# Modulations of the first layer summed on VectorE, and output weights split among the first projections: a two-layer hybrid attention and state-space block on one core

## The chip, the cores and the metric

The kernel runs on one core of a Trainium2 chip. The core has TensorE (matmuls into eight PSUM banks), VectorE, ScalarE and GpSimd, and queues on which transfers are issued. The metric is the device time of one execution in microseconds (us). TensorE's clock has two levels, 1.2 and 2.4 GHz; the profile gives the granted share of the higher one.

## The reference

A trunk of two layers works on 512 latent tokens (stream 0) and 256 context tokens (stream 1) of width 1024, side by side as 768 columns. Cut to what matters here:

```python
for l in range(DEPTH):                        # 2 layers
    m  = split(silu(c)     @ w_mod[l] + b_mod[l], 6)   # six modulations of 1024 for the latent tokens
    mc = split(silu(c_ctx) @ w_mod[l] + b_mod[l], 6)   # and six for the context tokens
    p  = modulate(rmsnorm(h,  g_norm1[l]), m[0],  m[1])  @ w_in[l]
    pc = modulate(rmsnorm(hc, g_norm1[l]), mc[0], mc[1]) @ w_in[l]
    oa, ob, om, od = neighbourhood(p, pc), sliding_window(p, pc), latent_attention(p, pc), state_space(p, pc)
    h  = h + m[2] * (concat(oa, ob, om, od) @ w_out[l])
    h  = h + m[5] * (square(relu(modulate(rmsnorm(h, g_norm2[l]), m[3], m[4]) @ w_mlp1[l])) @ w_mlp2[l])
    # the context stream hc goes the same way with mc, but not in the last layer
```

The weights `w_mod[l]` are 1024 x 6144 and `w_out[l]` is 1024 x 1024. So the modulations are two vectors (latent and context) times a large matrix, done once a layer. The first layer's m[0] and m[1] are needed before its first projection; m[2] is needed at the output projection, m[3] to m[5] in the MLP.

## The kernel before

**Matmuls in three products.** Every large fp32 matmul is done with split operands: a weight tile of 128 x 1024 (`wr`) is copied to a rounded high part by ScalarE (`wh`, L238) and the rest is subtracted by VectorE (`wl`, L239). `dense` (L250) then runs high x high, high x low and low x high on TensorE (L258). The pool of weights has three buffers each of `wr`, `wh` and `wl`; a load on SyncE's queue (SP) starts when its buffer is free.

**Stages of a layer.** After the first norm come the first projections (`ckv`, `cq` 0 and 1, `sq` 0), the latent queries and keys, and then three merges of generators, in which heads and projections take turns by numbers: latent heads with six more projections; sliding-window heads with the convolutions; the state-space scan with the neighbourhood heads and the first half of the output projection. Then comes the second half of the output projection, the second norm, and the MLP in four quarters of eight up blocks and eight down blocks. In the first layer the first projections run from 58.5 to 145.4 us, the latent heads to 212, the sliding-window heads to 350, scan and neighbourhood heads to about 470, and the MLP from some 500 to 1000 us. The order on each engine is set by a scheduler from the order of the program.

**Modulations.** Those of the first layer that its first norm needs, columns 0 to 2047, are made at the start by `first_mod`, which the change doesn't touch. The others of the first layer (columns 2048 to 6143) are `mod_steps(0)`: two groups of 2048 columns, eight steps each. A step loads two tiles of 128 x 1024 into the weight pool (L169, tag `wr`, shared with the projections) and multiplies them with the activated conditions on TensorE, into one bank that a group holds over its eight steps (L172). At the eighth step the bank is copied by ScalarE, transposed by TensorE and added to the bias. Steps stand in a list, `todo`; `more()` does the next of them: after each projection (`in_proj`, L705), while over `KEEP[0]` = 2 are left, and the last two in the merge with the scan. The second layer's modulations are made in the first layer's MLP by `mod_sums(1)` in another way: a chunk of 768 columns at a time, VectorE multiplies a weight tile with the condition of each of the two streams and adds it to one of two sums, over eight tiles (L206 for the first, L208 for the rest), and TensorE closes the chunk by multiplying the sums with ones (L212), a copy by ScalarE (L215) and three transposes (L221).

**Output weights ahead.** `split_ahead(l)` loads the eight blocks of `w_out[l]` (`wr`), splits them, and writes both parts by GpSimd's queue to a scratch in DRAM, `oscr` (L505). `wh` and `wl` are free when the writes have landed. In the first layer these eight are a third generator in the sliding-window merge; for the second layer they stand at the end of `todo`, behind all sums of modulations, in the first layer's MLP.

## Time and profile before

| | |
|---|---|
| median of 3 runs | 1813.32 us (1809.08 to 1813.66) |
| the profiled execution, its own time | 1818.32 us |
| its span | 1816.5 us |
| TensorE busy (share of the span) | 1756.8 us (97%) |
| VectorE busy | 1110.4 us (61%) |
| ScalarE busy | 737.2 us (41%) |
| GpSimd busy | 237.9 us (13%) |
| moved by DMA | 238.94 MB, mean 132 GB/s |

Busy time is the sum over an engine's instructions of one profiled execution. In the rows below PE is TensorE, PEld its weight loads, DVE VectorE, ACT ScalarE, POOL GpSimd and SP SyncE; a q behind a name is the queue of its instructions. "x8" counts instructions that the view has put together, and a bracket at the end of a row tells the idle time before it and what ended that. A name like `wl<-wr,wh` is the tile written and the tiles read. Times of rows are us from the start of the span.

### The profile page before, as it was taken

How to read it: one execution, taken by the hardware profiler on the slowest of the kernel's cores; microseconds unless marked ns; L12 is line 12 of the kernel's file. 1: busy time of each engine (PE TensorE's matmuls, PEld its weight loads, DVE VectorE, ACT ScalarE, POOL GpSimd, SP SyncE). 2: the span in 40 equal slices, each digit the busy share in tenths (PEclk: the TensorE clock that was granted, in tenths of full speed). 3: DMA queues.
4: the chain of work that ended last, by engine and by line, in shares of the span. 5: the costliest groups of instructions: out<-in, count | busy, mean ns of one | idle time of the engine just before them, and what ended most of it. 6: DMA issues, size and time to landing. Idle time of an engine off the chain costs nothing.

```text
span 1816.5 us, 28898 instructions
## 1 busy us (share of the span) xinstructions
PE 1756.8 (97%) x11170; PEld 1498.3 (82%) x11170; DVE 1110.4 (61%) x2372; ACT 737.2 (41%) x1497; POOL 237.9 (13%) x367
## 2 busy tenths in 40 slices
PE   8999999999989999999999999999989999999998
PEld 7877867777878888888887998688867898888888
DVE  5448448688677566557554675657778663434345
ACT  4347546655344123123114543555544451323244
POOL 0102012134320000000001331100024300000002
PEclk8999999999989999999999999999999999999999
DMA  9440267632634444434348643111233543332333
GB/s 334 137 151 18 65 209 238 211 123 83 209 111 137 141 129 131 119 106 140 109 124 298 191 128 125 47 36 36 91 122 116 200 139 94 102 94 93 103 101 121
DMA packets 86249, 238.94 MB, mean 132 GB/s; under 512 B 9200, under 2 KB 17392, under 8 KB 86112
## 3 DMA queue, kind: packets, MB, share of 16 engines
q1 hardware_dynamic: 74976, 208.57, 36.6%
q0 software_dynamic: 7104, 24.33, 3.7%
q10 hardware_dynamic: 4032, 4.20, 0.7%
q8 instruction: 88, 1.44, 0.3%
q14 instruction: 49, 0.40, 0.1%
HBM read 214.52 MB, written 22.54 MB: 131 GB/s over the span
## 4 chain that ended last, share of the span: by engine, by line
PE 62%; issue 26%; DVE 5%; DMA 3%; ACT 2%; POOL 1%; SPq 0%; DVEq 0%; ACTq 0%; POOLq 0%
PE pt L258 42%; PE pt L476 4%; PE pt L470 3%; PE pS L663 2%; PE pS L428 2%; PE pS L415 2%; PE pt L172 1%; PE pt L663 1%; PE pt L293 1%; PE pt L930 1%; PE pS L1028 1%; DMA wr<-in_w_mlp_dram 1%; PE pt L861 1%; DVE wl L239 1%; ACT wh L238 0%
## 5 line engine op out<-in xcount | busy, mean ns | idle before, releaser
L238 ACT CAST wh<-wr 128x1024 fp32r<-128x1024 f32 x206 | 215.8, 1048 | 424.4 <-PE pt L258 302.6
L239 DVE TENSOR_TENSOR wl<-wr,wh 128x1024 fp32r<-128x1024 f32 x206 | 254.1, 1234 | 116.6 <-ACT wh L238 101.0
L258 PE MATMUL pt<-ah,wh 128*128 128x512 f32 (+1 forms) x1304 | 276.4, 354 | 5.8 <-ACT ah L343 2.8
L258 PE MATMUL pt<-ah,wl 128*128 128x512 f32 (+1 forms) x1304 | 269.0, 348 | 2.3 <-DVE wl L239 2.3
L258 PE MATMUL pt<-al,wh 128*128 128x512 f32 (+1 forms) x1304 | 269.2, 347 | 0.0
L258 PEld LDWEIGHTS pt<-ah,wh 128*128 128x128 f32 x1304 | 214.1, 191 | 45.3 <-ACT ah L343 4.0
L258 PEld LDWEIGHTS pt<-ah,wl 128*128 128x128 f32 x1304 | 215.1, 191 | 34.1 <-DVE wl L239 2.7
L258 PEld LDWEIGHTS pt<-al,wh 128*128 128x128 f32 x1304 | 213.4, 191 | 31.0 <-issue 1.9
L258 PE MATMUL pt<-hh,wh 128*128 128x256 f32 (+1 forms) x896 | 168.8, 330 | 0.0
L258 PE MATMUL pt<-hl,wh 128*128 128x256 f32 (+1 forms) x896 | 167.0, 329 | 0.0
L258 PE MATMUL pt<-hh,wl 128*128 128x256 f32 (+1 forms) x896 | 166.9, 329 | 0.0
L1281 DVE SCALAR_TENSOR_TENSOR h<-pt,mod,h 128x512 f32<-128x512 f32 (+1 forms) x112 | 66.4, 597 | 153.8 <-PE pt L258 153.6
L258 PEld LDWEIGHTS pt<-hh,wh 128*128 128x128 f32 x896 | 137.7, 189 | 18.5 <-issue 1.9
L258 PEld LDWEIGHTS pt<-hh,wl 128*128 128x128 f32 x896 | 138.1, 190 | 15.4
L258 PEld LDWEIGHTS pt<-hl,wh 128*128 128x128 f32 x896 | 138.1, 190 | 15.0
L208 DVE SCALAR_TENSOR_TENSOR ma<-wm,cact,ma 128x768 f32<-128x768 f32 x112 | 110.5, 1015 | 61.9 <-DMA wm<-in_w_mod_dram 61.8
L1271 ACT ACTIVATE r<-pt 128x512 f32<-128x512 f32 (+1 forms) x101 | 51.3, 508 | 222.0 <-PE pt L258 220.4
L1273 DVE TENSOR_TENSOR r<-r 128x512 f32<-128x512 f32 (+1 forms) x101 | 58.2, 578 | 123.1 <-ACT r L1271 123.0
L319 POOL TENSOR_TENSOR sq<-sq,sq 128x256 f32<-128x256 f32 x66 | 65.0, 985 | 431.7 <-ACT sq L315 431.1
L452 ACT ACTIVATE pr<-pr,m 128x512 f32<-128x512 f32 (+2 forms) x96 | 77.8, 811 | 45.9 <-DVE m L438 45.2
L258 PE MATMUL pt<-oh,wo 128*128 128x256 f32 (+1 forms) x576 | 95.9, 311 | 0.0
L258 PEld LDWEIGHTS pt<-oh,wo 128*128 128x128 f32 x576 | 81.1, 199 | 5.6 <-issue 1.9
(295 smaller groups left out, 2472.3 us busy)
## 6 DMA issues: line engine op xcount, KB each, us to landing
wr<-in_w_mlp_dram SPq DMA_DIRECT2D x154, 512.0 KB, 3.5
wo<-oscr SPq DMA_DIRECT2D x66, 512.0 KB, 4.6
wm<-in_w_mod_dram SPq DMA_DIRECT2D x80, 384.0 KB, 3.6
wr<-in_w_a_dram SPq DMA_DIRECT2D x36, 512.0 KB, 4.2
wm<-in_w_mod_dram SPq DMA_DIRECT2D x32, 512.0 KB, 4.2
wr<-in_w_out_dram SPq DMA_DIRECT2D x16, 512.0 KB, 4.2
oscr<-wh POOLq DMA_DIRECT2D x16, 512.0 KB, 4.6
oscr<-wl POOLq DMA_DIRECT2D x16, 512.0 KB, 6.0
```

The costliest lines, as they stand in the source:

```text
L208: V.scalar_tensor_tensor(a[:, :T], w, cact[:, k, i:i + 1], a[:, :T], ALU.mult, ALU.add)
L238: A.copy(wh, raw)
L239: low.tensor_tensor(wl, raw, wh.bitcast(F32), ALU.subtract)
L258: PE.matmul(ps[:, :n], w[:, k - k0, :], acts[k][a][:, c0:c0 + n], start=i == 0, stop=i == len(mm) - 1)
L319: G.tensor_tensor(sq[0][:, :n], sq[0][:, :n], q[:, :n], ALU.add)
L452: A.activation(pr[:, :off], src, AF.Exp, scale=-1.0 if tabs else sgn, bias=mcol, accum_out=s2[:, a:a + 1])
L470: PE.transpose(pt[:, i * P:(i + 1) * P], probs[a][:, (g0 + i) * P:(g0 + i + 1) * P], ident)
L476: last_mm = PE.matmul(pv[64 * a:64 * a + 64, :P], vt(a, t), pts[a][:, t * P:(t + 1) * P], start=t == 0, stop=t == nkt - 1)
L663: PE.matmul(acc[t], acts[k][a][:, t * P:(t + 1) * P], slabs[pc][w][:, kk, :], start=k == 0 and x == 0, stop=k == KD - 1 and x == 2)
L1271: A.activation(r[:, :n], ps, AF.Relu)
L1273: V.tensor_tensor(r2[:, :n], r[:, :n], r[:, :n], ALU.mult)
L1281: V.scalar_tensor_tensor(h[d][:, c0:c0 + n], ps, mod[:, 40 + d, s:s + 1], h[d][:, c0:c0 + n], ALU.mult, ALU.add)
```

## The change

**Sums instead of matmuls.** The first layer's other modulations (columns 2048 to 6143) are no longer steps of matmuls. `mod_steps` is gone, and `mod_sums` takes a first block: `mod_sums(0, 16)` has five chunks of 768 columns and a last one of 256, each of eight steps of sums on VectorE and the transposes as a ninth. In the first layer its weight tiles and sums are in the large pool `u` (40 buffers, shared with activations), in the second layer as before. After every projection `more(MPROJ)` does three entries of the list instead of one; what is left of it is done ahead of the neighbourhood tables, and no longer in the merge with the scan.

**Output weights.** The first layer's eight splits leave the sliding-window merge. Two each stand behind the projections `ckv`, `cq` 0, `cq` 1 and `sq` 0. The second layer's splits no longer stand behind all its sums: one follows every chunk.

```diff
-    def mod_steps(l):
...
-                        w = wp.tile([P, 1024], F32, tag="wr", name=nm("wm"))
-                        nc.sync.dma_start(w, D["w_mod"][l, k * P:(k + 1) * P, c0:c0 + 1024])
...
-                        PE.matmul(box["ps"][32 * g:32 * g + 32, :], cact[:, k, :],
-                                  ws[g // 2][:, (g % 2) * 512:(g % 2) * 512 + 512],
-                                  start=k == 0, stop=k == KD - 1)
...
+    def mod_sums(l, b0=0):
+        for at in range(b0, 48, 6):
+            nb = min(6, 48 - at)
...
+                    w = (wp.tile([P, T], F32, tag="wr", name=nm("wm")) if l else unit("u", nm("wm")))[:, :W]
+                    nc.sync.dma_start(w, D["w_mod"][l, k * P:(k + 1) * P, at * P:at * P + W])
                     if k == 0:
+                        box.extend(unit("pT" if l else "u", nm("ma"))[:, :W] for _ in range(2))
                     for i, a in enumerate(box):
                         if k == 0:
+                            V.tensor_scalar(a, w, cact[:, k, i:i + 1], None, ALU.mult)
                         else:
+                            V.scalar_tensor_tensor(a, w, cact[:, k, i:i + 1], a, ALU.mult, ALU.add)
...
-    todo = mod_steps(0)
+    todo = mod_sums(0, 16)
...
         def in_proj(g, i, sg, fn):
             dense(D["w_a"][l, BLK[g, i]], acts, sg, fn)
-            if len(todo) > KEEP[l]:
-                more()
+            more(MPROJ)
...
+        ahead = split_ahead(0) if l == 0 else []
+
+        def some():
+            for _ in range(2):
+                if ahead:
+                    ahead.pop(0)()
         proj("ckv", 0)
+        some()
         proj("cq", 0)
+        some()
         next(latent)
         proj("cq", 1)
+        some()
...
         proj("sq", 0)
+        some()
...
-              (calls(*[lambda i=i: conv(i) for i in range(6)], lambda: gate_z(0), lambda: gate_z(1)), CONVN[l]),
-              (calls(*(split_ahead(0) if l == 0 else [])), 11))
-        more(len(todo) - KEEP[l])
+              (calls(*[lambda i=i: conv(i) for i in range(6)], lambda: gate_z(0), lambda: gate_z(1)), CONVN[l]))
+        more(len(todo))
...
-        merge((ssd(), SSDN[l] + na_), (na(), na_), (calls(*outa), OUTN[l]), (calls(*[more] * len(todo)), MODN[l]))
+        merge((ssd(), SSDN[l] + na_), (na(), na_), (calls(*outa), OUTN[l]))
...
-            todo.extend(mod_sums(l + 1))
-            todo.extend(split_ahead(l + 1))
+            sums, ahead = mod_sums(l + 1), split_ahead(l + 1)
+            for i in range(0, len(sums), 9):
+                todo.extend(sums[i:i + 9])
+                todo.append(ahead.pop(0))
```

**VectorE, first projections of the first layer.** Before, from the split of the second query projection (`wl_883`, the weights of `cq` 1) to that of the next projection (`wl_1021`, those of `sq` 0). Between them are an eviction of the first query projection (`cq`) and the small steps of an inverse root (`ss`, `rs`, `rsv`, `rsq`):

```order
L239 TENSOR_TENSOR wl_883<-wr_880,wh_882 128x1024
L373 COPY cq_783<-pt_816 128x256
L296 TENSOR_SCALAR ss_867<-pt_860 128x6
L279 TENSOR_SCALAR rs_869<-ss_867 128x6
L280 SCALAR_TENSOR_TENSOR rsv_870<-rs_869 128x6
L281 TENSOR_TENSOR rsv_870<-rsv_870,ss_867 128x6
L282 SCALAR_TENSOR_TENSOR rsq_871<-rsv_870 128x6
L283 SCALAR_TENSOR_TENSOR rsv_870<-rsv_870 128x6
L284 SCALAR_TENSOR_TENSOR rs_869<-rsq_871,rs_869 128x6
L285 SCALAR_TENSOR_TENSOR rs_869<-rsv_870,rs_869 128x6
L239 TENSOR_TENSOR wl_1021<-wr_1018,wh_1020 128x1024
```

Now, the end of the same stretch. `ma` are the two sums of the first chunk, `wm` a tile of `w_mod`, `wl_1091` the split of `sq` 0, `wl_1163` and `wl_1171` splits of output weights, and `mod_94<-pt_994` the bias added to the chunk's closed result:

```order
L170 SCALAR_TENSOR_TENSOR ma_776<-wm_867,cact,ma_776 128x768
L170 SCALAR_TENSOR_TENSOR ma_777<-wm_867,cact,ma_777 128x768
L170 SCALAR_TENSOR_TENSOR ma_776<-wm_871,cact,ma_776 128x768
L170 SCALAR_TENSOR_TENSOR ma_777<-wm_871,cact,ma_777 128x768
L202 TENSOR_TENSOR wl_1091<-wr_1088,wh_1090 128x1024
L202 TENSOR_TENSOR wl_1163<-wr_1160,wh_1162 128x1024
L170 SCALAR_TENSOR_TENSOR ma_776<-wm_979,cact,ma_776 128x768
L170 SCALAR_TENSOR_TENSOR ma_777<-wm_979,cact,ma_777 128x768
L170 SCALAR_TENSOR_TENSOR ma_776<-wm_983,cact,ma_776 128x768
L170 SCALAR_TENSOR_TENSOR ma_777<-wm_983,cact,ma_777 128x768
L202 TENSOR_TENSOR wl_1171<-wr_1168,wh_1170 128x1024
L188 TENSOR_TENSOR mod_94<-pt_994,vec_82 128x6 x2
```

From the split of `cq` 1 to the last of these sums there are fourteen sums and four splits on VectorE now (`sq` 0's among them), where no sum stood; the rows show the last eight sums.

**TensorE, the same place.** Before, the end of `cq` 1 (`al_247,wh_882`), a step of modulations, the broadcasts of an inverse root (L305), a sum of squares (L293), two products of the state-space's time steps (`dta`), and the start of `sq` 0:

```order
L258 MATMUL pt_912<-al_247,wh_882 128x256
L172 MATMUL pt_774<-wm_938,cact 32x512 x2
L172 MATMUL pt_774<-wm_940,cact 32x512 x2
L305 MATMUL pS_946<-con,rs_869 128x128 x4
L305 MATMUL pS_952<-con,rs_869 128x128 x2
L293 MATMUL pt_960<-ones,s_184_956 128x1
L771 MATMUL pt_1006<-dta_706,con 128x24 x2
L772 MATMUL pt_1006<-dta_706,ones 128x48
L258 MATMUL pt_1024<-ah_232,wh_1020 128x512
```

Now the same, where L268 is the broadcast, L174 and L183 are the closing of the first chunk (the sums times ones, and the transposes of `msb`, the copied result), and L221 is a matmul of `dense`:

```order
L221 MATMUL pt_953<-al_247,wh_923 128x256
L268 MATMUL pS_1016<-con,rs_910 128x128 x4
L268 MATMUL pS_1022<-con,rs_910 128x128 x2
L174 MATMUL pt_987<-ma_776,ones 32x384 x2
L174 MATMUL pt_987<-ma_777,ones 32x384 x2
L183 MATMUL pt_994<-con,msb_992 128x128 x3
L256 MATMUL pt_1030<-ones,s_208_1026 128x1
L733 MATMUL pt_1076<-dta_706,con 128x24 x2
L734 MATMUL pt_1076<-dta_706,ones 128x48
L221 MATMUL pt_1094<-ah_232,wh_1090 128x512
```

The step of modulations is gone, and the closing of the chunk stands ahead of `sq` 0, which is the row with `wh_1090`.

**SP's queue, the same stretch.** Loads in the order of their issue, before: weights of the projections (`in_w_a`) and pairs of `w_mod` tiles:

```order
L244 DMA wr_784<-in_w_a_dram 128x1024
L169 DMA wm_842<-in_w_mod_dram 128x1024
L169 DMA wm_844<-in_w_mod_dram 128x1024
L244 DMA wr_880<-in_w_a_dram 128x1024
L169 DMA wm_938<-in_w_mod_dram 128x1024
L169 DMA wm_940<-in_w_mod_dram 128x1024
L244 DMA wr_1018<-in_w_a_dram 128x1024
L169 DMA wm_1076<-in_w_mod_dram 128x1024
L169 DMA wm_1078<-in_w_mod_dram 128x1024
L244 DMA wr_1161<-in_w_a_dram 128x1024
```

Now, with the first output weights (`in_w_out`):

```order
L207 DMA wr_805<-in_w_a_dram 128x1024
L207 DMA wr_875<-in_w_out_dram 128x1024
L207 DMA wr_883<-in_w_out_dram 128x1024
L163 DMA wm_774<-in_w_mod_dram 128x768
L207 DMA wr_921<-in_w_a_dram 128x1024
L207 DMA wr_1000<-in_w_out_dram 128x1024
L163 DMA wm_780<-in_w_mod_dram 128x768
L163 DMA wm_784<-in_w_mod_dram 128x768
L207 DMA wr_1008<-in_w_out_dram 128x1024
L163 DMA wm_863<-in_w_mod_dram 128x768
L163 DMA wm_867<-in_w_mod_dram 128x768
L163 DMA wm_871<-in_w_mod_dram 128x768
```

Between two projections' loads there are one or two loads of output weights, and one to three narrower tiles of `w_mod`, where a pair of wide ones stood.

## Rows read from the trace of the kernel before

**Rows 1.** The page's first part: busy us (share) and instructions of each engine.

```profile
PE 1756.8 (97%) x11170; PEld 1498.3 (82%) x11170; DVE 1110.4 (61%) x2372; ACT 737.2 (41%) x1497; POOL 237.9 (13%) x367
```

**Rows 2.** Busy us by engine in stretches, granted TensorE clock, DMA share, GB/s.

```profile
58.50:145.40 86.90, 86.69 (x478) 66.79 (x477) 37.83 (x94) 32.32 (x70) 6.63 (x12) 1.00 0.45 144
107.80:145.40 37.60, 37.39 (x173) 25.47 (x172) 20.07 (x33) 19.98 (x41) 1.29 (x2) 1.00 0.39 126
145.40:212.00 66.60, 66.35 (x517) 53.62 (x515) 49.03 (x145) 44.03 (x110) 13.61 (x29) 1.00 0.18 57
212.00:350.00 138.00, 133.44 (x910) 104.49 (x909) 89.25 (x215) 75.97 (x176) 18.16 (x43) 0.99 0.58 188
300.00:340.00 40.00, 37.55 (x250) 31.39 (x249) 36.38 (x85) 25.15 (x56) 6.68 (x13) 1.00 0.73 232
540.00:930.00 390.00, 389.37 (x2274) 340.09 (x2274) 243.88 (x330) 94.08 (x144) 0.00 (x0) 1.00 0.43 129
980.00:1000.00 20.00, 17.68 (x100) 15.14 (x99) 10.06 (x13) 8.82 (x14) 3.18 (x6) 1.00 0.90 316
```

**Rows 3.** First and last of four transfers in the chain, 240 to 321 us.

```profile
241.24 4.65 DMA wr<-in_w_a_dram
...
315.34 5.74 DMA oscr<-wl
```

**Rows 4.** TensorE's timeline in the first projections: start, us, line, operation.

```profile
81.72 1.07 PE L172 MATMUL pt<-wm,cact 128*32 128x512 f32 x8
...
95.12 2.09 PE L258 MATMUL pt<-ah,wh 128*128 128x512 f32 x8
...
107.92 1.05 PE L172 MATMUL pt<-wm,cact 128*32 128x512 f32 x4
108.91 4.13 PE L1028 MATMUL pS<-cq,wq 128*128 128x512 f32 x10
...
119.86 1.05 PE L172 MATMUL pt<-wm,cact 128*32 128x512 f32 x4
```

**Rows 5.** Modulation matmuls (L172) alone: TensorE's busy time in two stretches.

```profile
58.50:145.40 86.90, 8.47 (x48) 1.21 (x48) 1.00 0.45 144
145.40:350.00 204.60, 11.64 (x64) 1.65 (x64) 0.99 0.45 145
```

**Rows 6.** VectorE's splits and sums by line: busy us, mean ns of one.

```profile
L239 DVE TENSOR_TENSOR wl<-wr,wh 128x1024 fp32r<-128x1024 f32 x206 | 254.1, 1234 | 116.6 <-ACT wh L238 101.0 <-issue 13.6 <-DMA oscr<-wl 1.6
L208 DVE SCALAR_TENSOR_TENSOR ma<-wm,cact,ma 128x768 f32<-128x768 f32 x112 | 110.5, 1015 | 61.9 <-DMA wm<-in_w_mod_dram 61.8
...
L206 DVE TENSOR_SCALAR ma<-wm,cact 128x768 f32<-128x768 f32 x16 | 9.5, 617 | 3.8 <-DMA wm<-in_w_mod_dram 2.9 <-PE pt L212 0.9
```

**Rows 7.** TensorE's timeline at the end of the first layer's MLP.

```profile
957.01 0.85 PE L212 MATMUL pt<-ma,ones 128*32 128x384 f32 x8
959.18 0.55 PE L221 MATMUL pt<-con,msb 128*128 128x128 f32 x3 [1.31 <-ACT msb L215]
...
997.48 2.11 PE L258 MATMUL pt<-ah,wl 128*128 128x512 f32 x8 [2.32 <-DVE wl L239]
```

**Rows 8.** The page's DMA issues: count, KB each, us from issue to landing.

```profile
wm<-in_w_mod_dram SPq DMA_DIRECT2D x80, 384.0 KB, 3.6
...
wr<-in_w_out_dram SPq DMA_DIRECT2D x16, 512.0 KB, 4.2
...
oscr<-wl POOLq DMA_DIRECT2D x16, 512.0 KB, 6.0
```

**Rows 9.** VectorE's timeline in the first projections.

```profile
79.68 1.23 DVE L239 TENSOR_TENSOR wl<-wr,wh 128x1024 fp32r<-128x1024 f32 x1 [7.58 <-ACT wh L238]
...
94.29 1.14 DVE L981 SCALAR_TENSOR_TENSOR ckv<-ckv,vec,pS 128x512 f32<-128x512 f32 x2 [1.15 <-PE pS L305]
```

**Rows 10.** GpSimd's timeline in the sliding-window heads.

```profile
288.52 0.45 POOL L962 TENSOR_TENSOR nql<-sq,nqh 128x128 fp32r<-128x128 f32 x1 [2.44 <-ACT nqh L961]
...
313.98 1.38 POOL L962 TENSOR_TENSOR nql<-sq,nqh 128x128 fp32r<-128x128 f32 x1 [0.54 <-ACT nqh L961]
```

More of the change, by code (lines that the diff above doesn't have):

```diff
@@ L44 @@
 NVEC = _at
-KEEP = (2, 0)
-LAND = 0
-MQ = 0
+MPROJ = 3
 LOWU = (0, 0)
@@ L50 @@
 MV = (2, 1)
-MODN = (12, 20)
 NU = 40
@@ L192, in mod_sums, with step @@
-    def mod_sums(l):
-        steps = []
-        for ch in range(8):
+        for at in range(b0, 48, 6):
+            nb = min(6, 48 - at)
             box = []
             for k in range(KD):
-                def step(ch=ch, k=k, box=box):
-                    w = unit("pr", nm("wm"))[:, 0:T] if LAND else wp.tile([P, T], F32, tag="wr", name=nm("wm"))
-                    (nc.sync, G, nc.scalar)[MQ].dma_start(w, D["w_mod"][l, k * P:(k + 1) * P, ch * T:(ch + 1) * T])
+                def step(at=at, W=nb * P, k=k, box=box):
+                    w = (wp.tile([P, T], F32, tag="wr", name=nm("wm")) if l else unit("u", nm("wm")))[:, :W]
+                    nc.sync.dma_start(w, D["w_mod"][l, k * P:(k + 1) * P, at * P:at * P + W])
```

57 lines of the change are left out of this document (14 added, 43 removed).

## The prediction, made before the changed kernel was run

> **What bounds the kernel now.** I read the page's busy shares first, then the busy times stretch by stretch, then the chain of waits where TensorE has gaps, and last the rows of the instructions that come and go. TensorE is busy 97% of the span and VectorE 61% [rows 1], so work taken from TensorE looks like a gain and VectorE looks as if it had room. Both are averages. By stretch [rows 2], VectorE has 37.8 of 86.9 us in the first projections (58.5 to 145.4 us, up to the first latent attention), 49.0 of 66.6 in the latent heads (145.4 to 212), 89.3 of 138.0 in the sliding-window heads (212 to 350), and in 300 to 340 there it already has 36.4 of 40. A busy TensorE is also not TensorE at its peak: in 240 to 321 us the chain of waits [rows 3] runs through four transfers, 21.9 us in all, from a projection's weights (4.65 us) over an output weight to two writes of split output weights (the last 5.74 us), which must land before a buffer is free. These are the splits that the change moves. So the sliding-window stretch is held now by transfers and the buffers behind them, not by matmuls, and the question is what is last there once they are gone.
>
> **What goes.** Sixteen steps of modulations on TensorE. A step has 8 matmul records, and where it stands in one piece it takes 1.07 us; a piece of 4 records takes 1.05, 0.99 us from its start at 107.92 to that of the next work at 108.91 [rows 4]. By stretch there are 48 and 64 records [rows 5], so 6 steps before 145.4 us, 8 up to 350, and 2 after. Since steps in two pieces cost double, the busy times count [rows 5]: 8.5 and 11.6 us, and some 2 for the last two steps. In the queries (106 to 121 us) three of the first six stand in five pieces, one of them of 8 records, the last at 119.86 [rows 4].
>
> **What comes.** On VectorE, 16 instructions for each full chunk: two of 0.62 us and fourteen of 1.015 us [rows 6], 15.4 us. Five full chunks are 77 us; the last one is a third as wide, some 6 us as an estimate from the same rows by width. Each chunk also closes on TensorE: ones times the sums (0.85 us), a copy by ScalarE for which TensorE waits 1.31 us if nothing stands between, and transposes of 0.55 us [rows 7]: 2.7 us back to back, 1.4 with other work between; I take 2, a middle. Eight splits move from the sliding-window stretch to the first projections, each 1.23 us of VectorE [rows 6] and three transfers of 0.52 MB (one load, two writes by GpSimd's queue) [rows 8]. VectorE's total grows by 83 us, in the stretches where it was busiest.
>
> **First projections, 58.5 to 145.4 us.** By amount it fits: 37.8 + 8 x 1.23 + 30.8 for two chunks + 1.2 for one projection split that now stands earlier = 79.6 of 86.9 us. By order it does not. Before, the split for the second query projection (cq, 1) is at 79.68 us and TensorE starts the next projection (sq, 0) at 95.12 [rows 4, 9]. Now VectorE has in between fourteen sums (14.2), four splits (4.9) and the scaling of ckv (1.1 [rows 9]), 20.2 us without the small ones, before the first chunk's last sum; from 80.9 us that is 101.1. The closing of this chunk stands in TensorE's queue ahead of (sq, 0), and everything behind it waits: 101.1 + 0.85 + 1.31 + 0.55 = 103.8 us, 8.7 us later than before. The queries give back five pieces of 0.99, 5 us. Then VectorE needs its 20.1 us [rows 2] and a chunk of 15.4, 35.5 of the 37.6 us that this piece took, so nothing is made up, and the second closing (2 us) stands ahead of the first scores: 8.7 - 5 + 2 = 5.7. I take **+6**. Bounds: if VectorE had all its sums in its gaps, the steps go and two closings come, 4 - 8.5 = -4; if the small instructions and the heavier traffic count in full, +12. On traffic: the stretch moves 144 GB/s now [rows 2], 12.5 MB; eight loads and sixteen writes of 0.52 MB and sixteen loads of 0.39 MB come, twelve of 0.52 go [rows 8]: about 25 MB, 270 GB/s over 93 us, where 980 to 1000 us shows 316 at a share of 0.90 [rows 2]. It fits, with little to spare.
>
> **Heads, 145.4 to 350 us.** VectorE has 49.0 + 89.3 = 138.3 us. Four chunks' sums are 10.4 + 51.4 = 61.8 (of which the order puts the smaller part into the latent heads), and nine splits leave (8 x 1.23 and the early one, 11.0): 189.1 of 204.6 us. TensorE loses 11.6 us of steps and gets four closings, 8 us, which is little. What is mainly to be won is the waits for transfers, 21.9 us, and VectorE decides how much: at 100% busy the stretch would take 189.1, **-15**; at the 91% that 300 to 340 reaches now (36.4 of 40) 207.8, **+3**. I take the middle, 95%, 199 us: **-6**. The reason for more than 91% is that a sum waits for nothing but a weight tile that was asked for long ahead, so it fills gaps that scores and their evictions leave.
>
> **Neighbourhood heads and scan, 350 to 470 us.** Two steps go (2 us) with the old layout's transposes and copies: **-3**, between -5 and 0.
>
> **First layer's MLP.** Before, the second layer's splits stand two to a weight at the end; there TensorE waits 2.32 us at 997.48 for a split behind a write [rows 7], and 1.31 us for the copy at 959 with no matmul between. Now each split stands after a chunk and the transposes stand behind another block. **-4**, between -6 and -1. I cost the spread splits at nothing: 540 to 930 us has VectorE busy 243.9 of 390 [rows 2]; without that cover a split's 1.23 us would show each time, 10 us in all, which the free buffer of three makes unlikely.
>
> **Sum.** +6 - 6 - 3 - 4 = -7. The profiled execution took 1818.32 us (span 1816.5 and 1.8 around it); with -7 it is 1811.3, 0.4% less. The median of the runs shown, 1813.32, lies 5.0 below the profiled one, so the forecast is **1806** for the median.
>
> **Rivals.**
> *VectorE becomes the bound (slower).* The first projections take +12, the heads run at 91% for +3, the later parts give back 4: +11, median 1824. For it: VectorE's order above, where a wait of one instruction holds all that stands behind it, softmax and evictions of TensorE's banks included. Against it: 189.1 of 204.6 leaves 8%. It decides from a VectorE share of 93% in 145.4 to 350 us up. Chance 0.25.
> *VectorE keeps up (much faster).* Sums fill only gaps: -4 in the first projections, -12 in the heads (192.6 us left, of which VectorE's 189.1 are 98%), -4 later: -20, median 1793. For it: 21.9 us of transfers in the chain. Against it: the closing ahead of (sq, 0). Chance 0.18.
> *GpSimd is slowed by the sums (no change).* The low half of each query is a subtraction on GpSimd, 0.45 us at 288.52, but 1.38 at 313.98 [rows 10], while VectorE works on the convolutions, which like the sums read two tiles. If some fourteen of those in the heads meet a sum and take 0.6 us more, 8 us come back: -7 + 8 = +1, median 1814. Against it: not every query is waited for. Chance 0.15.
> The Trainium skill (SBUF — State Buffer, Who interferes with whom) states that a VectorE instruction with two inputs in SBUF and a GpSimd instruction that reads SBUF share one port pair, and that the second of the two blocks until the first is done. The trace's 1.38 us agrees with that, without proving it; by that rule every meeting costs up to one sum.
>
> **How the numbers follow.** The forecast has 0.42 with a range of its own from 1800 to 1813. Less than 0.3% (5.4 us) is about what a measurement of this kernel can't tell from no change. Faster by more: the keeping-up case 0.18 and 0.24 of the forecast's 0.42, together 0.42. Within it: the other 0.18 of the forecast and 0.13 of the GpSimd case, 0.31. Slower: 0.25 and 0.02, 0.27. The range from 1793 to 1824 reaches to the cases at both ends.
>
> **What would show it.** Right: (sq, 0) starts 6 to 11 us later than 95.12, behind a closing that waits for VectorE; the first latent scores some 6 us later; then no transfer of output weights in the chain between the heads, VectorE 92 to 97% busy there, and the first layer's heads end 3 us or so earlier than before; no gap at the end of the first MLP. Wrong, slower: VectorE waits on its own order, and the heads take 205 us or more. Wrong, faster: (sq, 0) at 97 or earlier, so that the weights of VectorE's rows were smaller than the order says. The forecast also falls if the sums wait for their weight tiles, which now come in the large pool of 40 buffers behind the projections' loads on the same queue.

## The result: slower by 3%

The changed kernel takes 1865.70 us (median of 4 runs, 1862.60 to 1869.74), the kernel before 1813.49 in the same measurement. The ratio is 1.0295, 95% interval 1.027 to 1.032: 52 us slower, where 7 us faster was forecast, and outside the range.

The page of the changed kernel, its first part and the second part's row of the granted clock (40 equal slices, in tenths):

```profile
PE 1760.4 (94%) x11098; PEld 1508.6 (81%) x11098; DVE 1184.1 (64%) x2476; ACT 738.7 (40%) x1501; POOL 242.1 (13%) x367
...
PEclk8979989889999999999999999999999999999999
```

TensorE is busy 94% of a span of 1864.2 us, where it was 97% of 1816.5 [rows 1]; VectorE went from 1110.4 to 1184.1 us, 74 us more (83 were forecast; the sums alone are 80.8 us). So the new work has its expected size. TensorE's idle time grew from 59.7 to 103.8 us, and that is most of the loss. Its busy time rose by 3.6 us, although 23.5 us of steps with their transposes went and only 17.9 us of closings came: the rest of its work took some 9 us longer, at a mean granted clock that fell from 0.981 to 0.965.

Where it was lost, by points that both traces have (start in us from the start of the span):

| point in the first layer | before | after | later by |
|---|---|---|---|
| square of `ckv` for its norm | 72.7 | 72.5 | -0.2 |
| fourth projection (`sq` 0) starts | 95.1 | 109.4 | 14.3 |
| first latent scores reduced | 145.4 | 168.3 | 22.9 |
| first sliding-window sink | 217.1 | 246.3 | 29.2 |
| scan starts | 357.7 | 417.3 | 59.6 |
| second norm | 493.8 | 550.0 | 56.3 |
| an up block in the MLP's fourth quarter | 945.9 | 999.2 | 53.3 |
| second layer's first norm | 1064.5 | 1114.0 | 49.4 |
| last MLP block of the second layer | 1758.4 | 1806.1 | 47.6 |

All of the loss arises between 73 and 417 us, 60 us, and some 12 come back later. The traces end 47.6 us apart and not 52, because the profiled execution before, 1818.32 us, lies some 5 above its median. Differences of 2 or 3 us in such a table say nothing: the run below with the second layer's splits alone has the same program as the kernel before up to the MLP, and its trace takes 2.8 us less from the first latent scores to the scan, and 2.8 less again from there to the second norm.

The stretches, with the columns of [rows 2]; the first row is of the kernel before:

```profile
145.40:357.70 212.30, 206.82 (x1500) 163.48 (x1500) 141.70 (x375) 126.35 (x305) 35.33 (x80) 0.99 0.46 151
...
57.70:168.30 110.60, 90.26 (x448) 70.03 (x448) 75.97 (x136) 41.33 (x79) 15.01 (x28) 0.86 0.63 232
168.30:417.30 249.00, 213.34 (x1476) 174.46 (x1476) 180.76 (x438) 118.61 (x299) 30.89 (x64) 0.91 0.26 85
80.00:100.00 20.00, 9.95 (x62) 8.71 (x61) 16.62 (x27) 4.30 (x5) 2.15 (x4) 0.80 1.03 412
100.00:120.00 20.00, 15.45 (x74) 11.77 (x75) 10.47 (x23) 5.95 (x9) 2.13 (x4) 0.69 0.71 255
```

From 168 to 417 us VectorE is busy 180.8 of 249 us, 73%: it has room, and is not the bound. TensorE has 213.3 of 249 with a granted clock of 0.91, where it had 206.8 of 212.3 and 0.99 before. TensorE's timeline shows what it waits for; a closing is L174.

```profile
89.13 0.82 PE L268 MATMUL pS<-con,rs 128*128 128x128 f32 x6
103.97 2.42 PE L174 MATMUL pt<-ma,ones 128*32 128x384 f32 x8 [14.02 <-DVE ma L170]
...
109.44 3.51 PE L221 MATMUL pt<-ah,wh 128*128 128x512 f32 x8
...
257.19 0.84 PE L174 MATMUL pt<-ma,ones 128*32 128x384 f32 x4 [1.87 <-DVE ma L170]
259.36 1.49 PE L174 MATMUL pt<-ma,ones 128*32 128x384 f32 x4 [1.33 <-DVE ma L170]
...
304.91 2.33 PE L174 MATMUL pt<-ma,ones 128*32 128x384 f32 x8 [6.19 <-DVE ma L170]
...
353.62 2.33 PE L174 MATMUL pt<-ma,ones 128*32 128x384 f32 x8 [10.53 <-DVE ma L170]
...
403.20 0.94 PE L174 MATMUL pt<-ma,ones 128*32 128x128 f32 x8 [5.50 <-DVE ma L170]
```

Six closings stand in TensorE's queue, and TensorE stands idle in front of five of them, 14.02 + 1.87 + 1.33 + 6.19 + 10.53 + 5.50 = 39.4 us, each time for `ma`, the sums of VectorE. (The second chunk's closing, at 161.86, met no wait.) Everything behind a closing in the queue waits with it: after the first one `sq` 0 starts at 109.44 (95.12 in [rows 4]). The eight matmuls of a closing take 2.33 to 2.42 us behind a long wait, where the same form took 0.85 [rows 7]. Part of that is a second wait: a closing's last four matmuls read the other of the two sums, which ends 0.9 us after the first, and start at 104.90. Part is the clock: one of these matmuls lasts 0.85 us, where it lasted 0.49 to 0.51 before. The first eight of `sq` 0 take 3.51 instead of 2.09 [rows 4]: the granted clock is 0.69 on the mean of 100 to 120 us, so part of that stretch runs at 1.2 and part at 2.4 GHz, after TensorE has stood still.

What made the sums late at the first closing, from the chain of work that ended last (start, us, what):

```profile
83.58 15.14 DMA wr<-in_w_out_dram
...
98.82 1.05 ACT wh L201
...
99.90 0.78 DVE wl L202
...
101.97 1.95 DVE ma L170 x2
```

The load of an output weight takes 15.14 us (the median of such loads was 4.2 [rows 8]), in a stretch where the transfers' share is 1.03 and 412 GB/s move. ScalarE's copy waits for it, then VectorE's split L202, and the last sums stand behind this split in VectorE's queue. At the fourth closing the last sums wait for no tile; they stand behind convolutions and a split in VectorE's queue. At the fifth a tile of `w_mod` comes on top of such work (VectorE's timeline):

```profile
301.90 3.79 DVE L170 SCALAR_TENSOR_TENSOR ma<-wm,cact,ma 128x768 f32<-128x768 f32 x4
...
350.60 3.80 DVE L170 SCALAR_TENSOR_TENSOR ma<-wm,cact,ma 128x768 f32<-128x768 f32 x4 [2.85 <-DMA wm<-in_w_mod_dram]
```

VectorE is idle 2.85 us for the tile, and then does four sums in a row, 3.80 us, while TensorE waits its 10.53 us; for the first 4.7 of these it was at a split, convolutions and softmax. The transfers of output weights are gone from the chain between 230 and 417 us, but three waits for `w_mod` tiles stand there now, 9.65 us in all. The first and the last:

```profile
345.21 5.36 DMA wm<-in_w_mod_dram
...
395.51 2.20 DMA wm<-in_w_mod_dram
```

### The profile page after: what moved, and what is told of

It reads as the page before. It is cut to its first block, busy times and chain, and to the rows that moved or that the text cites. A ratio compares the mean times of both kernels' runs of the same rounds, so it can differ in the third digit from the quotient of the medians.

```text
span 1864.2 us, 28920 instructions
## 1 busy us (share of the span) xinstructions
PE 1760.4 (94%) x11098; PEld 1508.6 (81%) x11098; DVE 1184.1 (64%) x2476; ACT 738.7 (40%) x1501; POOL 242.1 (13%) x367
## 4 chain that ended last, share of the span: by engine, by line
PE 84%; DVE 9%; DMA 4%; issue 2%; ACT 2%; POOL 0%; SPq 0%; ACTq 0%; DVEq 0%; POOLq 0%
PE pt L221 65%; PE pt L439 3%; PE pt L433 3%; PE pS L391 2%; PE pS L626 2%; DVE ma L170 2%; PE pS L378 1%; PE pt L174 1%; DMA wr<-in_w_out_dram 1%; DVE wl L202 1%; PE pt L256 1%; PE pS L990 1%; DVE pr L401 1%; DMA wm<-in_w_mod_dram 1%; PE pt L892 1%
## 5 line engine op out<-in xcount | busy, mean ns | idle before, releaser
L202 DVE TENSOR_TENSOR wl<-wr,wh 128x1024 fp32r<-128x1024 f32 x206 | 253.8, 1232 | 71.3 <-ACT wh L201 62.9
L221 PE MATMUL pt<-ah,wh 128*128 128x512 f32 (+1 forms) x1304 | 279.2, 356 | 4.8 <-ACT ah L306 3.4
L221 PE MATMUL pt<-al,wh 128*128 128x512 f32 (+1 forms) x1304 | 268.6, 347 | 0.0
L221 PE MATMUL pt<-ah,wl 128*128 128x512 f32 (+1 forms) x1304 | 266.6, 347 | 0.0
L221 PEld LDWEIGHTS pt<-ah,wh 128*128 128x128 f32 x1304 | 216.8, 193 | 45.7 <-ACT ah L306 4.6
L221 PEld LDWEIGHTS pt<-ah,wl 128*128 128x128 f32 x1304 | 214.4, 191 | 30.7 <-issue 0.2
L221 PEld LDWEIGHTS pt<-al,wh 128*128 128x128 f32 x1304 | 212.8, 190 | 30.7 <-issue 1.9
L170 DVE SCALAR_TENSOR_TENSOR ma<-wm,cact,ma 128x768 f32<-128x768 f32 (+1 forms) x196 | 184.4, 977 | 74.1 <-DMA wm<-in_w_mod_dram 73.8
L221 PE MATMUL pt<-hh,wh 128*128 128x256 f32 (+1 forms) x896 | 168.2, 330 | 0.0
L221 PE MATMUL pt<-hl,wh 128*128 128x256 f32 (+1 forms) x896 | 167.0, 329 | 0.0
L221 PE MATMUL pt<-hh,wl 128*128 128x256 f32 (+1 forms) x896 | 166.9, 329 | 0.0
L221 PEld LDWEIGHTS pt<-hh,wh 128*128 128x128 f32 x896 | 137.6, 189 | 17.7 <-issue 0.6
L221 PEld LDWEIGHTS pt<-hh,wl 128*128 128x128 f32 x896 | 138.0, 190 | 15.4
L221 PEld LDWEIGHTS pt<-hl,wh 128*128 128x128 f32 x896 | 138.1, 190 | 15.0
L221 PE MATMUL pt<-oh,wo 128*128 128x256 f32 (+1 forms) x576 | 94.3, 306 | 0.0
L221 PEld LDWEIGHTS pt<-oh,wo 128*128 128x128 f32 x576 | 79.2, 194 | 6.0 <-issue 1.9
```

The source lines that it names most:

```text
L170: V.scalar_tensor_tensor(a, w, cact[:, k, i:i + 1], a, ALU.mult, ALU.add)
L202: low.tensor_tensor(wl, raw, wh.bitcast(F32), ALU.subtract)
L221: PE.matmul(ps[:, :n], w[:, k - k0, :], acts[k][a][:, c0:c0 + n], start=i == 0, stop=i == len(mm) - 1)
```

## The experiments

The theory from these rows, of the **place**: a closing stands in TensorE's queue at a point where the scheduler took the sums for done; on the chip they are not, and TensorE pays the whole lateness, and then a low clock. Rivals: the **splits** (their traffic and buffers in the first projections make the loss), **VectorE's work** (the sums take its time), and **late tiles** (the sums wait for `w_mod`). Each time is a median beside the kernel before, measured together with it on one chip; its own median was 1809.8 to 1812.7 us there, and 1813.49 beside the changed kernel. So a difference between two versions that were measured apart is certain to 3 or 4 us only, and the ratios compare better.

### The four parts

**The splits alone.** The kernel before, with only this:

```diff
         proj("ckv", 0)
+        some()
         proj("cq", 0)
+        some()
         proj("cq", 1)
+        some()
         proj("sq", 0)
+        some()
...
-              (calls(*(split_ahead(0) if l == 0 else [])), 11))
```

> The kernel before with one part of the change: the first layer's eight output-weight splits stand two each behind the first four projections; the modulations stay matmuls on TensorE, the second layer's splits stay at the end. Theory of the place (TensorE stands at the closings of the chunks, which come in its queue before VectorE has the sums): no closings here, so within some 10 us of the kernel before, 1803 to 1823. Theory of the splits (their loads and writes crowd the first projections and that is what makes VectorE late): the 14 us that were lost at the fourth projection are lost here too, 1827 or more.

Measured: 1832.37 us, ratio 1.0120 (1.0095 to 1.0145), 22 us slower: the theory of the splits has its own loss. All of it arises in the first projections: the products of the time steps, just ahead of the fourth one, start at 115.27 us instead of 94.9. The chain there, and the engines by stretch (columns as in [rows 2]):

```profile
66.86 6.11 DMA wr<-in_w_out_dram
...
75.37 5.14 DMA wr<-in_w_a_dram
...
94.25 6.02 DMA wr<-in_w_a_dram
```

```profile
60.00:80.00 20.00, 13.41 (x78) 11.29 (x76) 8.77 (x32) 4.62 (x12) 4.01 (x8) 0.91 0.63 201
80.00:100.00 20.00, 14.82 (x74) 11.95 (x74) 6.00 (x13) 4.47 (x5) 4.31 (x8) 0.76 0.79 282
```

Loads in a row, each behind a buffer of the weight pool that must come free, with TensorE at 13.4 and 14.8 of 20 us. The transfers move 201 and 282 GB/s here, less than the 412 above.

**The sums alone.** The changed kernel with both layers' splits where they stood before:

```diff
         proj("ckv", 0)
-        some()
...
+              (calls(*(split_ahead(0) if l == 0 else [])), 11))
...
+            todo.extend(mod_sums(l + 1))
+            todo.extend(split_ahead(l + 1))
```

> The changed kernel with its sums for the first layer, but the splits of both layers where they stood before (sliding-window merge, end of the MLP). Theory of the place: the closings still wait, 30 us or more slower than before, 1843 to 1870. Theory of the splits: most of the loss is gone, 1815 to 1830.

Measured: 1871.03 us, 1.0334 (1.0316 to 1.0353): as slow as the change, and a little more. So the sums alone bring the loss, and the two losses don't add: the first closing waits 4.3 us here, without the loads of output weights, and 14.0 in the change, but two later ones wait 9.89 and 14.58. The theory of the splits falls as the explanation of the change.

**The second layer's splits alone.** The kernel before with

```diff
-            todo.extend(mod_sums(l + 1))
-            todo.extend(split_ahead(l + 1))
+            sums, ahead = mod_sums(l + 1), split_ahead(l + 1)
+            for i in range(0, len(sums), 9):
+                todo.extend(sums[i:i + 9])
+                todo.append(ahead.pop(0))
```

> The kernel before with only the second layer's splits set between its chunks in the first layer's MLP. Both theories: the MLP ends some 4 to 6 us earlier, as it does in the changed kernel beside the kernel before; 1807 to 1810. If it is the same as before, the gain seen in that stretch came from elsewhere.

Measured: 1805.54 us against 1810.73, 0.9972 (0.9957 to 0.9987), 5.2 us faster (10 runs). This part is a gain, and with it alone the kernel beats both.

**The closings later.** The changed kernel, with the closing and the transposes as one list entry that comes six entries after the chunk's last sum (the last chunk's has nothing behind it in the list and stays):

```diff
-                    if k == KD - 1:
+                    if k == KD - 1 and l:
+                        close(W, box)
...
+                if not l:
+                    close(2 * nt * P, box)
                 pt = pst()
...
+        if not l:
+            for i in range(len(steps) // 9 - 2, -1, -1):
+                steps.insert(9 * i + 8 + 6, steps.pop(9 * i + 8))
```

> The changed kernel with each closing of the first layer's chunks (ones times sums, copy, transposes) moved six list entries, that is two projections, later; sums, loads and splits stay. Theory of the place: TensorE's waits for sums (39.4 us over six closings) fall under 10 us, the low clock that follows them goes too, and the time is 1800 to 1820. Theory of VectorE's time or of late weight tiles: what is late stays late, at least half of the loss stays, 1838 or more. Theory of the splits: 1840 or more.

Measured: 1824.98 us, 1.0080 (1.0060 to 1.0101): 41 of the 52 us are back (39 by the ratios), with every sum, load and split still there. The time is 5 us above what the theory of the place gave, and 13 below what the rivals gave. TensorE's timeline (L178 is the closing in this kernel), and one row of VectorE's, the first chunk's last four sums:

```profile
99.61 4.50 PE L229 MATMUL pt<-ah,wh 128*128 128x512 f32 x16 [5.06 <-ACT wh L209]
...
103.22 3.80 DVE L170 SCALAR_TENSOR_TENSOR ma<-wm,cact,ma 128x768 f32<-128x768 f32 x4
...
128.93 0.85 PE L178 MATMUL pt<-ma,ones 128*32 128x384 f32 x8
...
297.05 0.85 PE L178 MATMUL pt<-ma,ones 128*32 128x384 f32 x8
...
360.68 0.72 PE L178 MATMUL pt<-ma,ones 128*32 128x128 f32 x8 [3.56 <-DVE ma L170]
```

The five closings that moved take 0.85 us with no wait before them, and only the last one, which can't be moved back, waits 3.56. The first chunk's sums are no earlier here: they end at 107.02 us, in the change at 104.84. So the place of the closing is what changed, not the sums.

The first of these rows is `sq` 0. With no closing ahead of it, it still waits 5.06 us for its own weights and starts at 99.61, where it started at 95.12 before. Of the 14.3 us in the table above, 4.5 are thus the crowded loads' and some 10 the closing's. The first latent scores come 9.5 us late in this run. What the remaining 14 us of loss are made of isn't shown in full.

### Is it one delay or several?

**The first closing later, and the others later.** As above, for the first chunk alone and for the second to fifth (the sixth's stays at the end):

```diff
+            steps.insert(14, steps.pop(8))
```

```diff
+            for i in range(len(steps) // 9 - 2, 0, -1):
+                steps.insert(9 * i + 8 + 6, steps.pop(9 * i + 8))
```

> The changed kernel with the closing of the first chunk alone moved six list entries later. In the changed kernel this closing waits 14.0 us, behind sums that stand behind a split whose load took 15.1 us. If each closing costs its own wait and the low clock behind it: 15 to 22 us of the loss go, time 1843 to 1851. If the queue behind it was held by the same load anyway (the fourth projection's weights): under 8 us, 1858 or more.

> The changed kernel with the closings of the second to sixth chunk moved six entries later, and the first one left. Their waits are 25.4 us. If costs are each closing's own: the rest of what late closings gave, 19 to 30 us, time 1835 to 1847, and the gains of this run and of the one with the first alone add to the 41 us of all six. If one early delay makes all later ones: under 10 us, 1856 or more.

Measured: 1850.03 us (1.0224, 1.0201 to 1.0247) and 1837.66 us (1.0150, 1.0132 to 1.0169), 15.7 and 28.0 us less than the change. Together 43.7, beside 40.7 for all five at once; by the ratios 12.9 and 26.3, together 39.2, beside 39.0. Each closing costs on its own. TensorE's timeline with the first one late,

```profile
286.49 2.33 PE L178 MATMUL pt<-ma,ones 128*32 128x384 f32 x8 [6.19 <-DVE ma L170]
...
334.83 2.33 PE L178 MATMUL pt<-ma,ones 128*32 128x384 f32 x8 [10.51 <-DVE ma L170]
...
382.85 0.95 PE L178 MATMUL pt<-ma,ones 128*32 128x128 f32 x8 [5.41 <-DVE ma L170]
```

and with the others late:

```profile
105.19 2.42 PE L178 MATMUL pt<-ma,ones 128*32 128x384 f32 x8 [14.52 <-DVE ma L170]
...
231.62 0.85 PE L178 MATMUL pt<-ma,ones 128*32 128x384 f32 x8
```

The three later waits are 6.19, 10.51 and 5.41 us with the first delay gone, as in the change (6.19, 10.53, 5.50). The first is 14.52 with the others gone.

### What makes the sums late

**Few sums.** The changed kernel without six of the eight sums of each first-layer chunk (this leaves out most of the modulations' products):

```diff
                     for i, a in enumerate(box):
+                        if not l and 0 < k < KD - 1:
+                            continue
```

> The changed kernel with six of the eight sums of each chunk of the first layer left out (those of the second to seventh weight tile; so the modulations are wrong), 67 us of VectorE's work; all tiles are loaded, closings and splits stay where they are. What makes the sums late? Theory of VectorE's work (the sums stand in its queue behind and before other work and take their time): the waits at the closings fall from 39 us to under 15, time 1835 or less. Theory of late tiles (the last tile of a chunk comes late, behind loads on the same queue that wait for a buffer): the last sum is as late as before, waits of 28 us or more, time 1850 or more.

**One load.** All eight sums of a first-layer chunk from its first weight tile (this changes the modulations):

```diff
+                    if l or k == 0:
+                        w = (wp.tile([P, T], F32, tag="wr", name=nm("wm")) if l else unit("u", nm("wm")))[:, :W]
+                        nc.sync.dma_start(w, D["w_mod"][l, k * P:(k + 1) * P, at * P:at * P + W])
+                        kept[0] = w
+                    w = kept[0]
```

> The changed kernel with one weight tile loaded for each chunk of the first layer instead of eight, and all eight sums taken from it (the modulations are wrong): 42 loads of up to 0.39 MB gone, all of VectorE's work stays. Theory of late tiles: waits at the closings under 15 us, time 1835 or less. Theory of VectorE's work: 28 us or more of waits stay, time 1850 or more.

Measured: 1827.73 us (1.0092, 1.0063 to 1.0121) and 1821.82 us (1.0056, 1.0038 to 1.0075). By their times, each run came out as the one theory said and against the other: either edit takes away 38 to 44 of the 52 us, so neither rival holds alone. By the waits, one load agrees (11.3 us in all, under 15), and few sums lies between its two expectations (20.9 us, neither under 15 nor over 28). The closings tell more. With few sums:

```profile
103.17 2.42 PE L176 MATMUL pt<-ma,ones 128*32 128x384 f32 x8 [13.51 <-DVE ma L172]
...
320.00 2.33 PE L176 MATMUL pt<-ma,ones 128*32 128x384 f32 x8 [2.81 <-DVE ma L172]
...
365.32 0.72 PE L176 MATMUL pt<-ma,ones 128*32 128x128 f32 x8 [2.73 <-DVE ma L172]
```

With one load:

```profile
95.14 2.50 PE L177 MATMUL pt<-ma,ones 128*32 128x384 f32 x8 [6.34 <-DVE ma L173]
...
317.96 1.49 PE L177 MATMUL pt<-ma,ones 128*32 128x384 f32 x4 [4.55 <-DVE s L422]
...
362.04 0.42 PE L177 MATMUL pt<-ma,ones 128*32 128x128 f32 x8
```

At the first closing the wait is 13.51 us with hardly any sums before it, and 6.34 with the loads gone: there the crowded loads make more of it than VectorE's work. At the later ones the waits fall from 6.19, 10.53 and 5.50 to under 3 us with few sums. With one load the third, fourth and sixth closing wait for nothing, and the fifth still waits 4.55 us for VectorE, which ends a sum at 317.8 (the row names the small instruction behind that sum). Tiles and work stand one behind the other there, and without either the sums come in time or nearly so. How much of a later wait is the tile's and how much the work's, these two runs don't divide, since each also lets the scheduler place closings anew.

**The tiles over GpSimd's queue.** In the changed kernel, and in the one with late closings:

```diff
-                    nc.sync.dma_start(w, D["w_mod"][l, k * P:(k + 1) * P, at * P:at * P + W])
+                    (nc.sync if l else G).dma_start(w, D["w_mod"][l, k * P:(k + 1) * P, at * P:at * P + W])
```

> The changed kernel with the first layer's weight tiles of the modulations loaded over GpSimd's queue instead of SP's, so that they no longer stand behind loads that wait for a weight buffer. If SP's order made the sums late (8.8 us of VectorE's idle time at sums is ended by such a tile): the waits at the closings fall to 20 us or less, time 1840 to 1850. If the lateness is VectorE's own order and the crowded stretch of loads at the start: waits of 33 us or more stay, 1858 to 1872. If GpSimd's queue, with its writes of output weights that wait, is the worse place: above 1872.

> Late closings and the tiles over GpSimd's queue together. Late closings alone took 1825 and lost 9 us around 330 us, where a tile stood on SP behind output weights that waited for a buffer, with VectorE waiting for it and the softmax behind. If that is what is left: 1808 to 1818. If GpSimd's queue brings no more than it costs: 1820 to 1830.

Measured: 1871.21 us (1.0324, 1.0308 to 1.0339) and 1833.21 us (1.0110, 1.0082 to 1.0138). GpSimd's queue is no better place for the tiles: 5.5 us above the change, within what was expected for no gain, and 8 above late closings (5 by the ratios, whose intervals overlap), 3 beyond what was expected. The first closing waits 3.6 us longer than in the change:

```profile
107.15 2.43 PE L174 MATMUL pt<-ma,ones 128*32 128x384 f32 x8 [17.63 <-DVE ma L170]
```

### Buffers, clock, and a version with both

**The steps behind the splits.** The splits alone lost 20 us in the first projections. Here the steps of modulations that stood there come after the later projections, two at a time:

```diff
-            if len(todo) > KEEP[l]:
-                more()
+            if l or g not in ("ckv", "cq") and (g, i) != ("sq", 0):
+                more(min(2, max(0, len(todo) - KEEP[l])))
```

> The run that moved the splits alone was 22 us slower, and lost 20 of it before the fourth projection ended. This kernel is the same, but the steps of modulations that stood in the first four projections stand two after each later one, so that their pairs of wide tiles no longer ask for the same three buffers as the projections' and the output weights. Theory of the shared buffers: the loss in the first projections falls under 8 us, time 1808 to 1822. Theory of the traffic (the loads and writes of the output weights alone fill the stretch): 15 us or more stay there, time 1826 or more.

Measured: 1813.84 us, 1.0008 (0.9991 to 1.0025), no change. By stretch:

```profile
60.00:80.00 20.00, 20.00 (x117) 17.99 (x115) 11.53 (x32) 7.98 (x14) 7.51 (x14) 1.00 0.92 320
80.00:100.00 20.00, 20.00 (x128) 18.00 (x128) 12.27 (x31) 8.58 (x13) 3.89 (x8) 1.00 1.01 393
```

TensorE is full, at 393 GB/s: the traffic itself was no obstacle. The pairs of wide tiles and the output weights had fought for the three buffers: with the splits alone, SP's loads waited 15.5 us for the steps' matmuls between 58 and 115 us, here for none. This run shows something else: its scan starts 0.5 us earlier than before, its first latent scores 0.8, both too little to tell from nothing. So the heads, whose chain no longer has a transfer of output weights in it, gained at most about what the six steps moved there cost TensorE, some 6 to 8 us as an estimate from [rows 5].

**The splits so, and the second layer's too.** The edits of the last kernel and of the second layer's splits together.

> No sums in the first layer: its splits among the first projections with the steps on TensorE behind later projections (which alone was the same as before), and the second layer's splits between its chunks (which alone was 5 us faster). If the two add: 1803 to 1810, and the gain is the second part's alone; if freeing the sliding-window heads of transfers is worth what the waits in the chain showed (21.9 us before): below 1800.

Measured: 1808.92 us, 0.9985 (0.9971 to 0.9999), 3.6 us faster, inside the first expectation: the second layer's part is the gain, the rest is nothing.

**Matmuls in the wait.** The changed kernel, with TensorE kept at work ahead of the first closing:

```diff
+                        if not l and at == 16:
+                            pd = pst()
+                            for i in range(16):
+                                PE.matmul(pd, ones, con[:, 0:512], start=i == 0, stop=i == 15)
                         ps, n = pst(), W // 2
```

> The changed kernel with sixteen matmuls of 512 columns that nothing reads ahead of the first closing, so that TensorE works during the 14 us in which it waited and its granted clock needn't fall. If the low clock behind the wait costs time (its closing took 2.4 us for what took 0.85 before, granted clock 0.69 from 100 to 120 us): 5 to 9 us less, 1856 to 1861. If loads and VectorE hold the queries anyway: no change, 1862 to 1869; if the added matmuls come too late or too long: slower.

Measured: 1857.30 us, 1.0252 (1.0229 to 1.0276), with more work 8.4 us less than the change, or 7.8 by the ratios, whose intervals just touch (the change's begins at 1.027). One stretch, and TensorE's timeline:

```profile
100.00:120.00 20.00, 18.05 (x87) 11.81 (x86) 11.88 (x26) 6.34 (x9) 2.13 (x4) 1.00 0.75 265
```

```profile
92.28 13.89 PE L175 MATMUL pt<-con,ones 128*128 128x512 f32 x32
...
106.76 0.84 PE L178 MATMUL pt<-ma,ones 128*32 128x384 f32 x4
108.78 0.84 PE L178 MATMUL pt<-ma,ones 128*32 128x384 f32 x4 [1.18 <-DVE ma L170]
```

The granted clock stays at 1.00 where it was 0.69, and the first half of the closing takes 0.84 us, where it took 1.50 (103.97 to 105.47). The number is the expected one, but not at the place: the fourth projection starts at 111.85 and the first latent scores come at 168.5 (168.3 in the change), so in the first projections nothing was gained, as loads and VectorE hold the queries. The gain arises between 168 and 246 us (the first sliding-window sink comes at 241.3 instead of 246.3). There too the granted clock differs: 1.00 from 220 to 250 us, where the change has 0.66 in 220 to 230 and 0.83 in 240 to 250. But the scheduler has also placed that work in another order on VectorE and ScalarE, so the run doesn't show what a low clock costs, and the reason for the gain stays open.

**Late closings, spread out.** Two list entries after a projection, and the two chunks that only the MLP needs in the MLP (with their tiles in the weight pool, as in the second layer), to see if what late closings lose goes too:

```diff
-MPROJ = 3
+MPROJ = 2
-MV = (2, 1)
+MV = (3, 1)
...
-        more(len(todo))
+        more(len(todo) - (18 if l == 0 else 0))
...
+            if qd == 0 and l == 0:
+                more(len(todo) - n_next)
```

> The kernel with late closings, with two list entries after a projection instead of three, and with the two chunks that only the MLP's second half of a block needs (the sixth modulation) made in the first layer's MLP. Theory of the place, with VectorE's share in the heads as what is left of the loss (9 us at the latent keys, 9 us around the flush ahead of the neighbourhood tables): both losses go, time 1797 to 1808, faster than both kernels. If VectorE's work anywhere costs what TensorE's steps cost: 1812 or more.

Measured: 1826.15 us, 1.0077 (1.0054 to 1.0099): no better than late closings, a miss. Up to the end of the sliding-window heads it is level with the kernel before (the last sink comes at 339.7 us, 340.3 before); then it loses 13 us. On SP's queue, on VectorE and on TensorE:

```profile
320.62 1.47 SPq L485 DMA_DIRECT2D wo<-oscr  x2
322.35 25.77 SPq L163 DMA_DIRECT2D wm<-in_w_mod_dram  x4
```

```profile
329.03 1.95 DVE L170 SCALAR_TENSOR_TENSOR ma<-wm,cact,ma 128x768 f32<-128x768 f32 x2 [3.48 <-DMA wm<-in_w_mod_dram]
```

```profile
335.73 0.47 PE L441 MATMUL pt<-con,pr 128*128 128x128 f32 x1 [6.01 <-ACT os L342]
```

A `w_mod` tile is issued behind two loads of split output weights (`wo`), one of which waited 10.0 us for a buffer; VectorE stands 3.48 us at the sum for it, with softmax and evictions behind, and TensorE stands 6.01 us at a transpose whose source, through ScalarE, waits for these. The sums lose time in VectorE's queue as the closings do in TensorE's.

## Why the prediction was wrong

**The closings were costed by their own length.** This is the step that failed. "TensorE loses 11.6 us of steps and gets four closings, 8 us, which is little" took 2 us for each. Measured: their waits in the heads are 25.4 us beside that, and moving four of the later closings alone gave back 28.0 us (26.3 by the ratios). A step on TensorE needs only its tiles; a closing needs the last of sixteen instructions of another engine, and whatever is late there falls on everything behind it. The first closing was seen as such a wait, the others were not, although they stand in the queue in the same way. Heads and latent heads together were to give 6 us; from the first latent scores to the scan they lost 36.7.

**VectorE's share doesn't decide.** The heads were forecast by 91 to 100% of VectorE; it is busy 73% there. The rival "VectorE becomes the bound" had the right sign and was priced at +11 by the same reasoning: its 93% were never reached, but its sentence for it, that a wait of one instruction holds all behind it, is what happened. It was used for the first closing only. The last of its signs of being wrong, that the sums wait for their tiles, came true in part: VectorE stands 8.8 us for `w_mod` tiles up to the second norm.

**A slip in the sum.** Four chunks' sums stand in the heads' sum as 61.8 us. By the prediction's own weights three full chunks and the short one are 3 x 15.4 + 6 = 52.2, so VectorE's need was 179.5 us and not 189.1. The same reasoning at 95% would then have forecast -16 instead of -6: the slip didn't make the error, it hid part of it.

**First projections.** Here the last sum was forecast to end at 101.1 us, with the closing right behind it; the closing came at 103.97. That instant is nearly right, for a partly wrong reason: VectorE's weights alone were counted, and the run with few sums still waits 13.51 us. What held it was the split behind a load of 15.14 us; from 70.66 to 89.16 us SP issues the weights of `cq` 1 and `sq` 0, four output weights and seven tiles. The step on traffic ("270 GB/s over 93 us ... It fits, with little to spare") used a mean; in 80 to 100 us it was 412 GB/s. Forecast were +8.7 at the fourth projection and +6, with a bound of +12, at the first latent scores; measured are +14.3 and +22.9. The 5 us that the queries were to give back did not appear.

**The transfers in the chain.** "What is mainly to be won is the waits for transfers, 21.9 us": they went from the chain, and were not won. The splits alone, with no transfer at all in the chain from 200 to 350 us, came 23.5 us late to the first latent scores and 21.3 to the scan, a gain of 2 us that two executions of one program differ by. The 21.9 us were also those of one execution. In the trace of the second layer's splits alone, where the program up to there is that of the kernel before, the chain from 240 to 321 us goes through two transfers, 7.2 us:

```profile
290.44 3.36 DMA oscr<-wh
...
308.03 3.80 DMA oscr<-wh
```

With 14.7 us less of them it is 2.8 us faster from the first latent scores to the scan. Other waits stand beside those in the chain.

**GpSimd's low halves.** The median of the queries' subtractions in the sliding-window heads went from 0.46 to 0.58 us. The twelve of them take 10.2 us instead of 8.5, all forty-eight of the first layer 31.0 instead of 27.9, and none stands in the chain between 230 and 417 us. This rival falls by its size. The page's rule (the Trainium skill, SBUF — State Buffer, Who interferes with whom) was cited for it; the longest one, 2.10 us beside 1.38 [rows 10], agrees with a shared port, without proving it. One reading was wrong: VectorE was at a split of a weight at 313.98 (313.82 to 315.04), not at the convolutions. A split also reads two tiles, so the rule isn't touched; the one of 2.10 us, at 256.39, stands beside a sum and then a split.

**Right, one of them by chance.** The scan and neighbourhood heads gave back 3.3 us (59.6 to 56.3), forecast 3. That isn't shown: the second layer's splits alone, with the program of the kernel before in this stretch, take 2.8 us less there too, and the sums alone, with the change's own merge, took 2.7 more. The first layer's MLP gave back 5.9 (55.3 us late at its first block, 49.4 at the second layer's norm), forecast 4. That holds: the run with this part alone gained 5.8 there and 5.2 in all, and the sums alone, without this part, 0.8. The spread splits cost nothing there, and the transposes stand between two blocks:

```profile
1001.86 0.49 PE L183 MATMUL pt<-con,msb 128*128 128x128 f32 x3
```

## What to carry to other kernels

Work moved from TensorE to VectorE leaves a joint on TensorE where the result comes back; cost that joint by when the other engine's last instruction ends in its own queue (with the loads that it stands behind), not by its length, and put it some work later in the program: two projections later gave back some 40 of 52 us here. An engine with room on average (73%) can still be the one that is waited for. And a transfer in the chain of waits tells where time was spent in one execution, not what its removal gives.

## What was not expected of the hardware

The same load, 0.52 MB, took 4.2 us as a median and 15.14 us when 412 GB/s were moving. After a wait of 14 us the granted clock was 0.69 on the mean of 100 to 120 us, and a matmul of 128x384 took 0.85 us instead of 0.49 to 0.51; with matmuls that nothing reads in the wait it was 1.00 and the time 8.4 us less, though not in the stretch where the clock had been low, and with another order of the work behind. Two executions of one program had 21.9 and 7.2 us of transfers in the chain of the same stretch.
